# ConvFFN up-projection: weight sums and token operands between VectorE and GpSimd, and the PSUM banks of the GLA's output projection

## The chip, the cores and the metric

The kernel runs on one NeuronCore of a Trainium2 chip. Its engines are TensorE (matmuls), VectorE, ScalarE and GpSimd (element-wise work), and SyncE, which issues the DMAs. Each engine works through its own queue in order, and semaphores make one wait for another. The metric is the device time of one execution in microseconds (us), the median of several runs. "PE", "DVE", "ACT", "POOL" and "SP" in the profile are TensorE, VectorE, ScalarE, GpSimd and SyncE; "PEld" is TensorE's weight load.

## The reference

Two layers of a hybrid diffusion backbone in float32 over 1024 latent tokens and 256 context tokens, D = 1024. Layer 0 mixes tokens by a Fourier mixer beside a bidirectional gated linear attention (GLA), layer 1 by grouped-query attention; each is followed by a ConvFFN. What matters here:

```python
def conv_ffn(h, w_up, w_conv, b_conv, w_down):
    u = dwconv_centred(h @ w_up, w_conv, b_conv)     # 1024 -> 2 x 2816, three taps over tokens
    g, v = jnp.split(u, 2, axis=-1)
    return (jax.nn.silu(g) * v) @ w_down

# layer 0
y = jnp.concatenate([fourier_mix(u_f), o], axis=-1) @ w_out      # o: output of the GLA
h_lat = h_lat + ga1 * o_lat
f_lat = rms_norm(h_lat, g_norm_ffn[i]) * (1 + sc2) + sh2
h_lat = h_lat + ga2 * conv_ffn(f_lat, w_ffn_up[i], w_ffn_conv[i], b_ffn_conv[i], w_ffn_down[i])
```

## The kernel before, in words

**Products in three matmuls.** Each float32 operand is split into a high part, a rounded copy made by ScalarE (`split`, L208), and a low part, the subtraction that is left (`tt`, L204). A product is three matmuls of such parts (`mm3`): low times high, high times low, high times high. A group of matmuls needs the low part first, so it waits for the subtraction, which runs on VectorE (`V`) or GpSimd (`G`) as the call of `split` says.

**FFN up.** The product `h @ w_up` is a 2 x 2 block product in seven multiplications instead of eight (`PRODS`). Its token operands (B11, T1, B21, B22, T2, T4, T3) are blocks of the normed tokens and differences of them. `ffn_ops` makes them once for each half of the tokens (`hf` 0 and 1; n = 640 tokens a half in layer 0, 512 in layer 1; each block has u = n/2 columns). Its weight operands (A11, S1, A12, S2, S4, A22, S3) are made for each of the 22 blocks of 128 columns (f). `Up.load` loads two tiles of 8 x 128 columns (L1217), `Up.sums` makes three sums of halves of them, and `Up.split` makes the difference for S4 and splits all seven. All these are instructions on 128x512 elements. One (f, which halves) is a visit; layer 0 has 25 and layer 1 has 24, most of them over both halves.

**One step** (`up_step`) is one f and one half: seven groups of 12 matmuls into four PSUM banks X, V, W and Z. X takes A11's group, is copied out by ScalarE (L1307), and goes on accumulating with S2's group, so S2's first matmul waits for that copy. The other copies and additions out of PSUM (L1309 to L1319) are ScalarE's and VectorE's. `up_conv` then does the convolution of the step before: ScalarE's L1333 (centre tap) and L1335 (SiLU), and two VectorE instructions for the other taps (L1338 and L1339, or L1343 and L1345). The columns go to DRAM (L1352).

**Buffers.** The weights use ten slots (`W`): seven operands of the visit in work, and the two loaded tiles and the sums of the next. A slot comes free when the last half has used an operand, and `pump` then lets the next visit's work go on.

**Before the first FFN up** the GLA's half of the output projection runs (`out_part(4, 4, ...)`): for each half and each of the eight blocks n two PSUM tiles of 320 columns, each of 12 matmuls. VectorE adds each tile to the residual stream (`resid`, L918), which frees its bank. The banks go round in the group `MB = (0, 3)`, the first three; the first FFN-up visits go round in the group (0, 5). After each block of the second half, `h_done` does two steps of `ffn_ops` for the first half; those for the second half run as `side` within FFN up. Layer 1 has the same in `att_out(1, first)`, the attention's output projection, beside `ffn_ops` of the first half and the first visits' weights.

**What sets the order.** In the FFN TensorE's order is that of the code (`manual_schedule`). VectorE, ScalarE, GpSimd and the DMAs are ordered by a planner, which goes by the streams' priorities, the order of the code and its own reckoning of when each instruction is ready.

Of the kernel before, what the change touches and what calls it, by code (L numbers as in the profile page):

```python
# [15 lines left out]
ALU = mybir.AluOpType  # L16
# [88 lines left out]
def tile_hybrid_dit(  # L105
# [12 lines left out]
    V = nc.vector  # L118
    A = nc.scalar
    G = nc.gpsimd  # L120
# [82 lines left out]
    def tt(out_, a, b, op, eng=None):  # L203
        return (eng or V).tensor_tensor(out_, a, b, op)  # L204
# [39 lines left out]
    MB, XB, GB = (0, 3), (3, 1), (4, 4)  # L244
# [898 lines left out]
    def ffn_ops(N, ops, ring_p=None):  # L1143

        u = N.n // 2

        def put(name, p, src, eng):
            b = S((2, 2, u), True)
            split(src, b[:, 0], b[:, 1], eng)
            ops[name][p] = b  # L1150
        t0, t1 = N.hp[:2], N.hp[2:]
        b11, b12, b21, b22 = [[t[:, :, i * u:(i + 1) * u] for t in ts] for ts in (t0, t1) for i in range(2)]
        for p in range(2):
            N.scale(p)
            yield
            N.scale(p + 2)
            yield
            put("B11", p, b11[p], G)
            yield
        for p in range(2):  # L1160
            tt(b11[p], b12[p], b11[p], ALU.subtract)
            put("T1", p, b11[p], V)
            yield
        for p in range(2):
            put("B21", p, b21[p], G)
            yield
        for p in range(2):
            ring_t = [SM(2 * u).rearrange("p (k n) -> p k n", k=2) for _ in range(1)] if p == ring_p else None
            put("B22", p, b22[p], V)
            t3 = ring_t[0] if ring_t else b12[p]  # L1170
            tt(t3, b22[p], b12[p], ALU.subtract, G)
            yield
            tt(b22[p], b22[p], b11[p], ALU.subtract)
            put("T2", p, b22[p], V)
            yield
            if ring_t:
                t0[p].free()
                put("T3", p, t3, G)
                yield
                t4 = SM(2 * u).rearrange("p (k n) -> p k n", k=2)  # L1180
                tt(t4, b21[p], b22[p], ALU.subtract)
                t1[p].free()
                put("T4", p, t4, G)
            else:
                tt(b21[p], b21[p], b22[p], ALU.subtract)
                put("T4", p, b21[p], G)
                t1[p].free()
                yield
                put("T3", p, b12[p], G)
                t0[p].free()  # L1190
            yield
# [11 lines left out]
    class Up:  # L1203
# [18 lines left out]
        def sums(self):  # L1222
            r, tmp = self.r, self.tmp
            lo, hi = slice(0, 4), slice(4, 8)
            e = self.sum_on
            tt(tmp[:, lo], r[1][:, lo], r[1][:, hi], ALU.add, e)
            tt(tmp[:, hi], tmp[:, lo], r[0][:, lo], ALU.subtract, e)
            tt(r[1][:, lo], r[0][:, lo], r[1][:, lo], ALU.subtract, e)

        def split(self, M):  # L1230

            r, tmp = self.r, self.tmp
            lo, hi = slice(0, 4), slice(4, 8)
            src = dict(A11=r[0][:, lo], S2=tmp[:, hi], S3=r[1][:, lo], S1=tmp[:, lo], A12=r[0][:, hi], A22=r[1][:, hi], S4=r[0][:, lo])
            for a, _, _ in PRODS:
                b = M((2, 4, P), True)
                split(src[a], b[:, 0], b[:, 1], V if a in self.on_v else G)
                self.w[a] = b
                if a == "A11":
                    tt(r[0][:, lo], r[0][:, hi], tmp[:, hi], ALU.subtract, G)  # L1240
                elif a == "S2":
                    tmp.free()
                elif a == "S3":
                    r[1].free()
                elif a == "S4":
                    r[0].free()
                yield

    V1 = (("S3", "S1", "A12"), ("S3", "S1", "A12"))
    V2 = (("S3", "S1", "A12"), ("S3", "S1", "A12"))  # L1250
    S1 = (G, G)

    class Ups:


        def __init__(self, l, single):
            self.visits = [(f, (0,)) for f in range(single)]
            for f in range(single, NF):
                self.visits.append((f, (0, 1)))
                if f < 2 * single:  # L1260
                    self.visits.append((f - single, (1,)))
            self.made = [Up(l, f) for f, _ in self.visits]
            for i, up in enumerate(self.made):
                up.on_v, up.sum_on = (V1[l], S1[l]) if i < 2 * single + 1 else (V2[l], G)
            self.gen = self.prep(self.made[1:], W)

        def prep(self, ups, M, after=None):
# [394 lines left out]
    with stream(1):  # L1662
        for hf in range(2):
            go_load(hf)
            go_dump(0, hf)
            go_dump(1, hf)
        S.join(GM)
        run(ups.prep(ups.made[:1], S, gl[1, 1].f[:, 1, HALF - 1:HALF]))
        out_part(4, 4, lambda k, hf: (gh[k // 2, hf][:, k % 2, :], gl[k // 2, hf][:, k % 2, :]), MB, h_done,
                 lambda: pump(ups.gen, (W, 1)))  # L1670
    if "mem" in dbg:
        print("least S", S.low, "W", W.low, "GM", GM.low)
# [447 lines left out]
```

## Time and profile before

| | |
|---|---|
| time, median of 3 runs | 3104.79 us (3103.47 to 3115.6) |
| the profiled execution | 3111.55 us, its span 3109.8 us |
| TensorE busy | 2812.2 us, 90% |
| VectorE busy | 2332.2 us, 75% |
| ScalarE busy | 1448.9 us, 47% |
| GpSimd busy | 1535.5 us, 49% |
| first FFN up | about 722 to 1330 us |
| second FFN up | about 2310 to 2830 us |

All times within the kernel are from the start of the span of the profiled execution. A busy share is a mean over the span. In a row of a timeline, "[2.09 <-ACT t L1307]" says that the engine stood idle for 2.09 us before the instruction and that ScalarE's line 1307 ended the wait; "x3" says that three instructions of one kind followed each other without a gap. L204 is the line of the helper `tt` and L208 that of `split`'s copy, so most element-wise work carries these two lines, and one tells the instructions apart by engine, shape and time.

### The profile page before, as it was taken

How to read it: one execution, taken by the hardware profiler on the slowest of the kernel's cores; microseconds unless marked ns; L12 is line 12 of the kernel's file. 1: busy time of each engine (PE TensorE's matmuls, PEld its weight loads, DVE VectorE, ACT ScalarE, POOL GpSimd, SP SyncE). 2: the span in 40 equal slices, each digit the busy share in tenths (PEclk: the TensorE clock that was granted, in tenths of full speed). 3: DMA queues.
4: the chain of work that ended last, by engine and by line, in shares of the span. 5: the costliest groups of instructions: out<-in, count | busy, mean ns of one | idle time of the engine just before them, and what ended most of it. 6: DMA issues, size and time to landing. Idle time of an engine off the chain costs nothing. (4 is left out here: it accounts for less than half of the span.)

```text
span 3109.8 us, 52191 instructions
## 1 busy us (share of the span) xinstructions
PE 2812.2 (90%) x20047; PEld 2680.2 (86%) x20047; DVE 2332.2 (75%) x3729; ACT 1448.9 (47%) x2896; POOL 1535.5 (49%) x1229
## 2 busy tenths in 40 slices
PE   6999987897899999997989899999977999998888
PEld 3999977796899999997989889989867989998788
DVE  7897489869776666768674788868788778887774
ACT  3544433435444444442353546646655444544333
POOL 2025273127554444467874753343377555554661
PEclk7999978898999999998999999999998999999899
DMA  8553202321344434387733220020231222228763
GB/s 275 180 167 100 96 31 94 127 99 48 104 141 128 128 110 128 100 268 233 246 108 116 89 82 11 28 92 21 75 92 58 78 73 67 77 77 272 235 214 108
DMA packets 375790, 371.28 MB, mean 119 GB/s; under 512 B 15579, under 2 KB 305011, under 8 KB 375540
## 3 DMA queue, kind: packets, MB, share of 16 engines
q1 hardware_dynamic: 374482, 365.88, 37.1%
q8 instruction: 157, 2.57, 0.3%
q10 hardware_dynamic: 1058, 2.07, 0.2%
q14 instruction: 93, 0.76, 0.1%
HBM read 282.95 MB, written 84.93 MB: 118 GB/s over the span
## 5 line engine op out<-in xcount | busy, mean ns | idle before, releaser
L154 PE MATMUL psum<-t,t 128*128 128x256 f32 (+4 forms) x17896 | 2615.2, 306 | 208.2 <-DVE t L204 77.5
L154 PEld LDWEIGHTS psum<-t,t 128*128 128x128 f32 x17896 | 2490.8, 196 | 296.6 <-DVE t L204 91.0
L204 POOL TENSOR_TENSOR t<-t,t 128x512 fp32r<-128x512 f32 (+8 forms) x736 | 1077.6, 1479 | 866.1 <-ACT t L208 523.3
L204 DVE TENSOR_TENSOR t<-t,t 128x512 fp32r<-128x512 f32 (+13 forms) x760 | 808.8, 1092 | 168.3 <-ACT t L208 123.6
L208 ACT CAST t<-t 128x512 fp32r<-128x512 f32 (+5 forms) x857 | 555.4, 670 | 648.8 <-POOL t L204 182.9
L204 POOL TENSOR_TENSOR t<-t 128x512 f32<-128x512 f32 (+3 forms) x265 | 327.7, 1254 | 390.4 <-ACT t L664 157.4
L204 DVE TENSOR_TENSOR t<-t,psum 128x320 f32<-128x320 f32 (+4 forms) x416 | 202.9, 508 | 126.4 <-PE psum L154 94.3
L1333 ACT ACTIVATE t<-t,cvs 128x639 f32<-128x639 f32 (+3 forms) x176 | 153.1, 870 | 153.4 <-DVE t L204 142.5
L208 ACT CAST t<-psum 128x512 fp32r<-128x512 f32 (+4 forms) x248 | 130.7, 536 | 134.2 <-PE psum L158 60.0
L158 PE MATMUL psum<-ident,t 128*128 128x128 f32 (+2 forms) x955 | 150.9, 280 | 38.7 <-DVE t L204 23.4
L1918 POOL TENSOR_SCALAR t<-t,ring 128x640 f32<-128x640 f32 x128 | 101.6, 807 | 170.4 <-DVE ring L1908 80.7
L204 DVE TENSOR_TENSOR t<-psum,t 128x512 fp32r<-128x512 f32 (+4 forms) x248 | 151.3, 615 | 37.0 <-ACT t L208 33.9
L158 PEld LDWEIGHTS psum<-ident,t 128*128 128x128 f32 (+2 forms) x955 | 113.1, 143 | 47.8 <-DVE t L204 27.6
L918 DVE SCALAR_TENSOR_TENSOR t<-psum,mods,t 128x256 f32<-128x256 f32 (+2 forms) x208 | 91.9, 473 | 62.7 <-PE psum L154 53.2
L1907 DVE TENSOR_REDUCE ring<-psum 128x1 f32<-128x640 f32 x128 | 104.5, 817 | 20.0 <-PE psum L154 14.4
L1909 ACT ACTIVATE t<-psum,ring 128x640 f32<-128x640 f32 x128 | 102.3, 800 | 25.6 <-DVE ring L1908 11.9
L1335 ACT ACTIVATE t<-t 128x511 f32<-128x511 f32 (+3 forms) x88 | 60.4, 686 | 82.2 <-DVE t L1339 45.7
L204 DVE TENSOR_TENSOR ring<-ring 128x1 f32<-128x1 f32 (+5 forms) x296 | 76.2, 259 | 20.8 <-ACT ring L1912 12.8
L1313 ACT COPY t<-psum 128x320 f32<-128x320 f32 (+1 forms) x88 | 35.2, 400 | 121.2 <-PE psum L154 121.2
L1338 DVE SCALAR_TENSOR_TENSOR t<-t,cvs 128x641 f32<-128x641 f32 (+1 forms) x44 | 52.0, 1182 | 47.3 <-ACT t L1333 47.3
L1343 DVE SCALAR_TENSOR_TENSOR t<-t,cvs 128x255 f32<-128x255 f32 (+1 forms) x66 | 53.7, 840 | 44.5 <-ACT t L1333 44.5
L338 DVE SCALAR_TENSOR_TENSOR t<-t,scv,t 128x256 f32<-128x256 f32 x168 | 80.1, 527 | 3.1 <-DMA t<-in_w_mod_dram 2.9
(144 smaller groups left out, 1672.7 us busy)
## 6 DMA issues: line engine op xcount, KB each, us to landing
t<-in_w_ffn_up_dram SPq DMA_DIRECT2D x98, 512.0 KB, 3.9
ring<-in_w_mod_dram SPq DMA_DIRECT2D x56, 512.0 KB, 4.0
t<-in_w_ffn_down_dram SPq DMA_DIRECT2D x96, 256.0 KB, 5.5
t<-in_w_even_in_dram SPq DMA_DIRECT2D x28, 512.0 KB, 4.7
t<-in_w_ffn_down_dram SPq DMA_DIRECT2D x72, 192.0 KB, 3.8
t<-y_d SPq DMA_DIRECT2D x20, 640.0 KB, 5.9
t<-in_w_mod_dram SPq DMA_DIRECT2D x96, 128.0 KB, 2.2
t<-in_w_ffn_down_dram SPq DMA_DIRECT2D x24, 512.0 KB, 4.5
```

The costliest lines, as they stand in the source:

```text
L154: cls.keep(out_, nc.tensor.matmul(out_, *args, **kw).ins)
L158: cls.keep(out_, nc.tensor.transpose(out_, *args).ins)
L204: return (eng or V).tensor_tensor(out_, a, b, op)
L208: A.copy(hi, src)
L338: behind(V.scalar_tensor_tensor(a, r, s, a, ALU.mult, ALU.add))
L918: last_resid[0] = V.scalar_tensor_tensor(h[:, n % 2, a:b], ps[:, a - c0:b - c0], mods[:, l, m, n, v:v + 1], h[:, n % 2, a:b], ALU.mult, AL ...
L1333: A.activation(x, c[:, j, at:at + m], AF.Identity, bias=tap(l, 3, ft), scale=tap(l, 1, ft))
L1335: A.activation(us[0], us[0], AF.Silu)
L1343: V.scalar_tensor_tensor(x[:, s0 + 1:e], c[:, j, 2 + s0:1 + e], tap(l, 0, ft), x[:, s0 + 1:e], ALU.mult, ALU.add)
L1907: V.tensor_reduce(mx[:, i:i + 1], ps, AX.XY, ALU.max)
L1909: A.activation(pt[:, i * HALF:(i + 1) * HALF].rearrange("p (b n) -> p b n", b=2), ps, AF.Exp, bias=nb[:, i:i + 1], scale=SCALE, accum_out= ...
L1918: G.tensor_scalar(pt[:, i * HALF:(i + 1) * HALF], pt[:, i * HALF:(i + 1) * HALF], ex[:, i:i + 1], 1.0, ALU.mult, ALU.mult)
```

## The change

In `Up.sums` the three weight sums go from GpSimd to VectorE, and so does the difference for S4 in `Up.split`. Which weight splits run on VectorE is now one list, `ON_V`, in place of lists by layer and visit; it names the same three operands as these did. In `ffn_ops` the split of B11, the difference for T3 and the split of T4 go from GpSimd to VectorE, and the split of B22 from VectorE to GpSimd. The GLA's output projection takes its PSUM tiles from the group (0, 5) in place of (0, 3).

```diff
--- before.py
+++ after.py
@@ -1155,7 +1155,7 @@
             yield
             N.scale(p + 2)
             yield
-            put("B11", p, b11[p], G)
+            put("B11", p, b11[p], V)
             yield
         for p in range(2):
             tt(b11[p], b12[p], b11[p], ALU.subtract)
@@ -1166,9 +1166,9 @@
             yield
         for p in range(2):
             ring_t = [SM(2 * u).rearrange("p (k n) -> p k n", k=2) for _ in range(1)] if p == ring_p else None
-            put("B22", p, b22[p], V)
+            put("B22", p, b22[p], G)
             t3 = ring_t[0] if ring_t else b12[p]
-            tt(t3, b22[p], b12[p], ALU.subtract, G)
+            tt(t3, b22[p], b12[p], ALU.subtract)
             yield
             tt(b22[p], b22[p], b11[p], ALU.subtract)
             put("T2", p, b22[p], V)
@@ -1180,10 +1180,10 @@
                 t4 = SM(2 * u).rearrange("p (k n) -> p k n", k=2)
                 tt(t4, b21[p], b22[p], ALU.subtract)
                 t1[p].free()
-                put("T4", p, t4, G)
+                put("T4", p, t4, V)
             else:
                 tt(b21[p], b21[p], b22[p], ALU.subtract)
-                put("T4", p, b21[p], G)
+                put("T4", p, b21[p], V)
                 t1[p].free()
                 yield
                 put("T3", p, b12[p], G)
@@ -1222,10 +1222,9 @@
         def sums(self):
             r, tmp = self.r, self.tmp
             lo, hi = slice(0, 4), slice(4, 8)
-            e = self.sum_on
-            tt(tmp[:, lo], r[1][:, lo], r[1][:, hi], ALU.add, e)
-            tt(tmp[:, hi], tmp[:, lo], r[0][:, lo], ALU.subtract, e)
-            tt(r[1][:, lo], r[0][:, lo], r[1][:, lo], ALU.subtract, e)
+            tt(tmp[:, lo], r[1][:, lo], r[1][:, hi], ALU.add)
+            tt(tmp[:, hi], tmp[:, lo], r[0][:, lo], ALU.subtract)
+            tt(r[1][:, lo], r[0][:, lo], r[1][:, lo], ALU.subtract)
 
         def split(self, M):
 
@@ -1234,10 +1233,10 @@
             src = dict(A11=r[0][:, lo], S2=tmp[:, hi], S3=r[1][:, lo], S1=tmp[:, lo], A12=r[0][:, hi], A22=r[1][:, hi], S4=r[0][:, lo])
             for a, _, _ in PRODS:
                 b = M((2, 4, P), True)
-                split(src[a], b[:, 0], b[:, 1], V if a in self.on_v else G)
+                split(src[a], b[:, 0], b[:, 1], V if a in ON_V else G)
                 self.w[a] = b
                 if a == "A11":
-                    tt(r[0][:, lo], r[0][:, hi], tmp[:, hi], ALU.subtract, G)
+                    tt(r[0][:, lo], r[0][:, hi], tmp[:, hi], ALU.subtract)
                 elif a == "S2":
                     tmp.free()
                 elif a == "S3":
@@ -1246,9 +1245,7 @@
                     r[0].free()
                 yield
 
-    V1 = (("S3", "S1", "A12"), ("S3", "S1", "A12"))
-    V2 = (("S3", "S1", "A12"), ("S3", "S1", "A12"))
-    S1 = (G, G)
+    ON_V = ("S1", "A12", "S3")
 
     class Ups:
 
@@ -1260,8 +1257,6 @@
                 if f < 2 * single:
                     self.visits.append((f - single, (1,)))
             self.made = [Up(l, f) for f, _ in self.visits]
-            for i, up in enumerate(self.made):
-                up.on_v, up.sum_on = (V1[l], S1[l]) if i < 2 * single + 1 else (V2[l], G)
             self.gen = self.prep(self.made[1:], W)
 
         def prep(self, ups, M, after=None):
@@ -1666,7 +1661,7 @@
             go_dump(1, hf)
         S.join(GM)
         run(ups.prep(ups.made[:1], S, gl[1, 1].f[:, 1, HALF - 1:HALF]))
-        out_part(4, 4, lambda k, hf: (gh[k // 2, hf][:, k % 2, :], gl[k // 2, hf][:, k % 2, :]), MB, h_done,
+        out_part(4, 4, lambda k, hf: (gh[k // 2, hf][:, k % 2, :], gl[k // 2, hf][:, k % 2, :]), (0, 5), h_done,
                  lambda: pump(ups.gen, (W, 1)))
     if "mem" in dbg:
         print("least S", S.low, "W", W.low, "GM", GM.low)
```

## Rows read from the trace of the kernel before

**Rows 1.** Busy time by stretch: the stretch and its length in us, then for each engine busy us and (x instructions), the granted TensorE clock as a share of full speed, the share of the DMA engines and GB/s.

```profile
690.00:734.00 44.00, 30.17 (x160) 28.59 (x160) 34.43 (x36) 24.65 (x42) 31.38 (x18) 0.84 0.16 57
734.00:802.00 68.00, 49.03 (x268) 47.05 (x268) 60.01 (x71) 37.30 (x60) 45.37 (x30) 0.80 0.17 54
802.00:1330.00 528.00, 524.93 (x3730) 490.12 (x3730) 372.54 (x496) 246.01 (x437) 247.16 (x208) 1.00 0.39 124
2250.00:2340.00 90.00, 69.01 (x370) 59.57 (x369) 73.94 (x72) 50.60 (x87) 72.77 (x46) 0.90 0.29 89
2340.00:2800.00 460.00, 419.02 (x3366) 414.20 (x3366) 369.86 (x432) 222.78 (x436) 267.35 (x215) 0.97 0.24 73
```

**Rows 2.** TensorE's waits, by who ended them: us in total, times, longest. The first row is of 690 to 734 us, the second of 734 to 802, the third of 2250 to 2340, the last two of 2340 to 2800.

```profile
PE psum L154 <- DVE t L918: 13.8, 4, 6.2
...
PE psum L154 <- POOL t L204: 10.4, 4, 4.4
...
PE psum L154 <- POOL t L204: 10.3, 5, 4.9
...
PE psum L154 <- ACT t L1307: 24.5, 15, 2.4
PE psum L154 <- POOL t L204: 12.9, 5, 3.4
```

**Rows 3.** Timeline of one visit of the second FFN up and the change to the next, 2581 to 2604 us: start, duration, engine, line, operation, tiles, shape, count, and the idle time before it with what ended it.

```profile
2581.24 0.38 SPq L1217 DMA_DIRECT2D t<-in_w_ffn_up_dram  x1
...
2585.11 3.01 POOL L204 TENSOR_TENSOR t<-t,t 128x512 f32<-128x512 f32 x2 [3.90 <-DMA t<-in_w_ffn_up_dram]
...
2591.06 1.89 DVE L1345 SCALAR_TENSOR_TENSOR t<-t,cvs 128x511 f32<-128x511 f32 x1
2591.09 4.70 POOL L204 TENSOR_TENSOR t<-t,t 128x512 fp32r<-128x512 f32 x3 [1.59 <-ACT t L208]
...
2592.86 3.48 DVE L204 TENSOR_TENSOR t<-t,t 128x512 fp32r<-128x512 f32 x2
...
2596.59 0.68 DVE L204 TENSOR_TENSOR t<-t,t 128x512 fp32r<-128x512 f32 x1
...
2599.33 1.66 DVE L1339 SCALAR_TENSOR_TENSOR t<-t,cvs,t 128x512 f32<-128x512 f32 x1
...
2601.02 0.63 ACT L1335 ACTIVATE t<-t 128x513 f32<-128x513 f32 x1 [1.73 <-DVE t L1339]
2601.32 1.26 POOL L204 TENSOR_TENSOR t<-t 128x512 f32<-128x512 f32 x1 [0.88 <-DVE t L204]
...
2602.78 0.35 ACT L1307 COPY t<-psum 128x256 f32<-128x256 f32 x1
...
2603.28 0.95 PE L154 MATMUL psum<-t,t 128*128 128x256 f32 x6 [2.09 <-ACT t L1307]
```

**Rows 4.** Groups of instructions by line and shape, 2340 to 2800 us: first GpSimd's sums of weights (three of a visit's four have the first form, the sum of two halves of one tile has the second), then three of VectorE's groups. Behind the count: busy us, mean ns of one, and the engine's idle time before them with what ended it.

```profile
L204 POOL TENSOR_TENSOR t<-t,t 128x512 f32<-128x512 f32 x63 | 96.1, 1539 | 91.7 <-DMA t<-in_w_ffn_up_dram 90.2
L204 POOL TENSOR_TENSOR t<-t 128x512 f32<-128x512 f32 x20 | 25.8, 1290 | 15.5 <-DMA t<-in_w_ffn_up_dram 7.4 <-DVE t L204 4.3 <-DVE t L1339 2.9
...
L204 DVE TENSOR_TENSOR t<-t,t 128x512 fp32r<-128x512 f32 x67 | 73.0, 1090 | 3.8 <-ACT t L208 3.8
...
L204 DVE TENSOR_TENSOR t<-t,t 128x511 f32<-128x511 f32 x20 | 34.5, 1723 | 0.0
L1345 DVE SCALAR_TENSOR_TENSOR t<-t,cvs 128x511 f32<-128x511 f32 x20 | 31.7, 1586 | 0.7
```

**Rows 5.** Timeline of the change from the output projection to the first FFN up, 700 to 733 us, columns as in rows 3.

```profile
700.67 1.57 POOL L204 TENSOR_TENSOR t<-t,t 128x640 fp32r<-128x640 f32 x1 [0.94 <-ACT t L208]
...
704.75 15.50 POOL L204 TENSOR_TENSOR t<-t,t 128x640 fp32r<-128x640 f32 x8
...
722.00 11.39 PE L154 MATMUL psum<-t,t 128*128 128x320 f32 x60 [6.18 <-DVE t L918]
...
725.01 0.81 DVE L204 TENSOR_TENSOR t<-t 128x640 f32<-128x640 f32 x1
...
725.71 4.79 POOL L204 TENSOR_TENSOR t<-t,t 128x512 fp32r<-128x512 f32 x3 [3.38 <-ACT t L208]
```

**Rows 6.** GpSimd's plain 128x512 differences and sums by shape, columns as in rows 4: two rows of 690 to 734 us, two of 734 to 802, two of 2250 to 2340.

```profile
L204 POOL TENSOR_TENSOR t<-t,t 128x512 f32<-128x512 f32 x3 | 5.4, 1805 | 0.0
...
L204 POOL TENSOR_TENSOR t<-t 128x512 f32<-128x512 f32 x1 | 1.8, 1796 | 0.8 <-DVE t L204 0.8
...
L204 POOL TENSOR_TENSOR t<-t,t 128x512 f32<-128x512 f32 x6 | 8.7, 1457 | 4.0 <-DMA t<-in_w_ffn_up_dram 3.9
L204 POOL TENSOR_TENSOR t<-t 128x512 f32<-128x512 f32 x3 | 5.0, 1682 | 10.0 <-DVE t L1345 7.1 <-DMA t<-in_w_ffn_up_dram 2.9
...
L204 POOL TENSOR_TENSOR t<-t,t 128x512 f32<-128x512 f32 x12 | 18.6, 1563 | 4.2 <-DMA t<-in_w_ffn_up_dram 2.1 <-DVE t L204 1.9
...
L204 POOL TENSOR_TENSOR t<-t 128x512 f32<-128x512 f32 x4 | 5.6, 1394 | 1.0 <-DMA t<-in_w_ffn_up_dram 1.0
```

**Rows 7.** Waits in 2340 to 2800 us by who ended them, columns as in rows 2: GpSimd's for weights, and VectorE's two for ScalarE.

```profile
POOL t L204 <- DMA t<-in_w_ffn_up_dram: 97.6, 29, 6.6
...
DVE t L1343 <- ACT t L1333: 34.8, 38, 1.1
DVE t L1338 <- ACT t L1333: 29.4, 34, 1.3
```

## The prediction

> **What bounds the kernel now.** The shares of the page (table above) are means over stages with different limits, so I begin with the busy times by stretch, over the two FFN-up stages and what leads into them [rows 1]. They show four different limits. In the steady part of the first FFN-up (802 to 1330 us) TensorE is busy 524.9 of 528 us: nothing that happens on VectorE or GpSimd there can be won back. In the run-up to it (690 to 734 and 734 to 802) TensorE idles 13.8 and 19.0 us, at granted clocks of 0.84 and 0.80. In the run-up to the second FFN-up (2250 to 2340) it idles 21.0 us, and in the second FFN-up itself (2340 to 2800), whose matmuls are 256 columns wide instead of 320, 41.0 us. Together that is 94.8 us, and it is all that the change can reach.
>
> Second view, who ends TensorE's waits in each stretch [rows 2]: between 690 and 734 it is the residual add on VectorE (L918), 13.8 us in four waits; between 734 and 802 and between 2250 and 2340 GpSimd ends 10.4 and 10.3 us; in the second FFN-up ScalarE's L1307 ends 24.5 us in 15 waits and GpSimd 12.9 us in five.
>
> L1307 copies the A11 product out of PSUM and takes 0.35 us, so it isn't slow itself. The third view, the timeline of one change of visit, shows why it is late [rows 3]: ScalarE works in order, L1307 (2602.78) stands behind L1335 (2601.02), L1335 has waited 1.73 us for the convolution on VectorE (L1339, 1.66 us), and before that VectorE had run contended splits since 2591.06. The two engines slow each other: a subtraction or product on 512 columns takes VectorE 0.68 us when GpSimd is idle (2596.59) and 1.74 us when it runs (2592.86, two in 3.48 us); it takes GpSimd 1.26 us alone and 1.57 us beside it (2591.09, three in 4.70 us). A pair that alone would cost 0.68 + 1.26 = 1.94 us takes 1.57 to 1.74 us together, 81% to 90% of the sum. I take 85%: what the two engines do between SBUF tiles goes nearly one after the other. So in these stretches it is the sum over both engines that counts, and VectorE does the same work in about half the time.
>
> The Trainium skill (SBUF — State Buffer, section "SBUF: two separate sides") says of this that VectorE instructions with two SBUF inputs and GpSimd instructions take a shared pair of ports as an exclusive lock for the whole instruction, so the sum would count in full. The rows show a little less than that; by the page the total below would be 38 us instead of 32, still the same case.
>
> **The change part by part.** *Weight operands.* Each visit prepares one column block of weights: three sums, a fourth difference for S4, and seven splits. Today the four sums run on GpSimd, of the splits A11, S2, S4 and A22 too, and S3, S1, A12 on VectorE. The new list of splits names the same three, so no split moves: GpSimd goes from eight instructions a visit to four, VectorE gets four more. The rows count them: in 2340 to 2800, 63 + 20 = 83 sums of 128x512 in plain f32 [rows 4], 20.75 visits. Each moved sum takes 1.26 us off GpSimd and puts 0.68 us on VectorE; of the shared time that saves 0.58 x 0.85 = 0.49 us.
>
> In the second FFN-up not all four count. Two of them (2585.11, x2) run in the half of the visit where TensorE doesn't wait; the first sum (2601.32) and the S4 difference (one of the three at 2591.09) lie in the loaded stretch that ends with TensorE's 2.09 us wait [rows 3]. So 2 x 0.49 = 0.98 us a visit, x 20.75 = 20 us, of the 41.0 us there. GpSimd's own five waits (12.9 us) should go as well, since its queue is half as long, but they are in the same 41 us and I don't add them. Bounds: nothing, or all of the 41 us; a loss is the third rival's.
>
> In the first FFN-up's steady part I take 0: TensorE hides it. Its cover is large: VectorE is busy 372.5 of 528 us there [rows 1], 71%.
>
> *Token operands.* Of the seven operands per half, B11's split, the T3 difference and T4's split go to VectorE and B22's split goes to GpSimd. There are two of each (p = 0, 1), so GpSimd loses a net four instructions per half and VectorE gets them. In the first layer they are 128x640: 1.57 us on GpSimd at 700.67, and 0.81 us on VectorE at 725.01 [rows 5]; each saves 0.76 x 0.85 = 0.65 us of shared time. In 690 to 734 there are also 3 + 1 weight sums, in 734 to 802 another 6 + 3 [rows 6]. That gives 4 x 0.65 + 4 x 0.49 = 4.6 us and 4 x 0.65 + 9 x 0.49 = 7.0 us, 11.6 us together. GpSimd is close to saturated there (eight instructions without a gap from 704.75, 15.5 us [rows 5]) and TensorE idles 32.8 us, but not every instruction lies ahead of one that it waits for; I take two thirds, 8 us. Bounds: 0 and 20.
>
> In 2250 to 2340 there are 12 + 4 plain differences [rows 6], T3's among them, and a net two splits: 18 x 0.49 = 8.8 us. GpSimd ends half of TensorE's idle time there (10.3 of 21.0), since the attention output weights are split behind this work. I take half, 4 us, between 0 and 10.
>
> *Five PSUM banks.* The GLA's part of the output projection uses banks 0 to 4 instead of 0 to 2, the group from which FFN-up then takes its own. A tile then waits for the L918 five tiles before it, not three. The four waits, 13.8 us, should mostly go, that at 722.00 (6.18 us) included. But TensorE only runs ahead to the next obstacle: the first visit of FFN-up needs all seven token operands, and the last GpSimd splits for it end at 730.5 (725.71 + 4.79) [rows 5], while TensorE gets through most of that visit by 733.4 (722.00 + 11.39). So by themselves the banks are worth 0 to 5 us; I count nothing beyond the 8 us.
>
> Sum: 20 + 8 + 4 = 32 us. The profiled execution took 3111.55 us, 1.75 us beyond its span of 3109.8 us; 3111.55 - 32 = 3079.6. The median of the runs is 6.8 us lower than the profiled one, so I forecast 3104.8 - 32 = 3073 us. Clock that comes back when the gaps close isn't counted.
>
> **The rivals.** *All of it comes.* If the two engines had been the only limit, TensorE saturates in the second FFN-up too: 41 us there, 11.6 + 8.8 us in the run-ups, 3044 us. For it: GpSimd's and L1307's waits have one origin. Against it: VectorE stays about as busy as before, and its queue is what L1307 waits for.
>
> *VectorE keeps what GpSimd gives up.* Four more instructions a visit are 4 x 0.68 = 2.7 us of VectorE time. What it gains is less contention: the 67 split subtracts at 1.09 us, the 20 products at 1.72 us and the 20 L1345 at 1.59 us [rows 4] lie above the 0.68 us of a free one by 27 + 21 + 18 = 66 us, 3.2 us a visit; with half of GpSimd's instructions gone, half of it, 1.6 us. By this count VectorE's load grows by 1.1 us a visit and the critical queue is no shorter; only the run-ups gain, 12 us: 3093 us, no change.
>
> *VectorE stands still for weights (slower).* The sums are the first readers of the loaded weights. GpSimd now waits 97.6 us for in_w_ffn_up in this stretch [rows 7], 4.7 us a visit, at no cost. On VectorE a sum at the head of the queue holds up the PSUM adds and the convolution behind it, ScalarE's L1333, L1335 and L1307 wait for those, and TensorE for L1307. VectorE has 369.9 / 20.75 = 17.8 us of work in a visit of 460 / 20.75 = 22.2 us; with 1.1 us more, and the 3.1 us that it already waits for L1333 (34.8 + 29.4 us [rows 7]), 22.0 us are spoken for. A new wait of more than about 1 us a visit decides. If half of GpSimd's wait, 2.35 us, lands there and half of that is absorbed, it costs 1.2 x 20.75 = 24 us; up to 45 us if none is. Less 12 us in the run-ups that is 3117 to 3138, say 3127 us. For it: the load lands 3.9 us after its issue (2581.24 to 2585.11 [rows 3]). Against it: VectorE has gaps of its own in each visit, those before L1333's results, into which the sums can fall, and the planner orders by what its own reckoning says is ready. The first layer has room for such a wait.
>
> *That the planner, which orders every engine but TensorE here, moves something unrelated* can add or take some 10 us to any of these.
>
> **How the numbers follow.** My case (about 3073, its own range 3058 to 3088) has 0.45, all of it 0.15, VectorE keeps it 0.23, VectorE waits 0.17. About 0.5%, 15.5 us, is what a measurement can tell from no change, so faster means under 3089 and slower over 3120. The first two are faster; of the second rival a tenth or so is faster by chance, and of the third a quarter stays within the band: faster 0.62, same 0.24, slower 0.14. The range 3036 to 3118 leaves out the far end of the first rival and the upper half of the third.
>
> **What would show it.** Right: in the second FFN-up GpSimd's instructions halve, TensorE's waits for GpSimd are gone, those for L1307 fall to about half, and the mean of VectorE's 128x512 split falls from 1.09 towards 0.8 us; in 690 to 734 no waits for L918; in 802 to 1330 no difference. Wrong: rows in which VectorE waits for in_w_ffn_up by more than 20 us in total; TensorE's waits for L1307 as long as before; or a difference in stages that the change does not touch.

## The result, and the profile after

The kernel after takes 3085.54 us (median of 6 runs, 3078.85 to 3093.69) beside 3106.18 us for the kernel before on the same chip: ratio 0.9929 [0.9913, 0.9945], about 22 us. The forecast was 3073 us, 3058 to 3088 for the likeliest case. The profiled execution took 3089.33 us, its span 3087.4 us.

Where the 22.3 us between the two spans come from, by the start of the same instruction in both traces (the copies of A11's product, L1307 before and L1302 after, are numbered from 0 in each FFN up, two per visit):

| stretch | before, us | after, us | difference | forecast |
|---|---|---|---|---|
| middle of the output projection to copy 10 of the first FFN up | 632.0 to 890.9 | 632.1 to 880.4 | -10.6 | -8 |
| from there to its last copy, 43 | to 1342.0 | to 1330.2 | -1.2 | 0 |
| to copy 10 of the second FFN up | to 2445.3 | to 2417.8 | -15.7 | -4 |
| to its copy 43 | to 2814.0 | to 2792.1 | **+5.6** | **-20** |
| to the end | to 3109.8 | to 3087.4 | -0.5 | 0 |

So the sum is near, but the two run-ups bring 26 us instead of 12, and the steady second FFN up, which should have brought most, has become slower. (The forecast's 20 us were for 2340 to 2800 us, 20.75 visits; copies 10 to 43 are 16.5 visits, for which the same 0.98 us a visit make 16 us.) The busy times by stretch of the kernel after, which answer to [rows 1], the stretches moved with the stage:

```profile
690.00:734.00 44.00, 32.05 (x178) 30.73 (x177) 39.38 (x52) 28.17 (x47) 23.59 (x10) 0.78 0.21 69
734.00:802.00 68.00, 51.76 (x318) 50.48 (x317) 63.41 (x89) 39.94 (x66) 26.24 (x20) 0.87 0.17 54
802.00:1320.00 518.00, 515.18 (x3668) 480.78 (x3667) 369.82 (x568) 242.15 (x430) 123.35 (x122) 1.00 0.39 125
2236.00:2326.00 90.00, 67.86 (x370) 58.88 (x369) 75.64 (x88) 51.36 (x86) 48.22 (x30) 0.89 0.29 89
2326.00:2786.00 460.00, 425.97 (x3418) 420.06 (x3416) 376.73 (x531) 225.00 (x447) 134.78 (x129) 0.97 0.26 79
```

GpSimd's instructions fall to about six tenths: of a visit's eight on the weights four are left, and its other work has stayed. In the steady first FFN up TensorE is busy 515.2 of 518 us, as before. TensorE's waits, which answer to [rows 2], the first row of 690 to 734 us, the second of 734 to 802, the third of 2236 to 2326, the last two of copies 10 to 43 of the second FFN up:

```profile
PE psum L154 <- DVE t L204: 11.9, 4, 4.5
...
PE psum L154 <- DVE t L204: 14.4, 2, 8.3
...
PE psum L154 <- POOL t L204: 12.0, 4, 7.4
...
PE psum L154 <- ACT t L1302: 22.2, 19, 2.0
PE psum L154 <- DVE t L204: 5.2, 1, 5.2
```

The waits for L918 and, in the first run-up, for GpSimd are gone; waits for VectorE's L204, which makes the operands now, stand in their place. In the second run-up GpSimd still ends 12.0 us. In the second FFN up the waits for GpSimd are gone too, but those for the A11 copy are not: 22.2 us, against 23.7 us in the same copies before. The same 33 copies in one row each, the kernel before first (columns as in [rows 1]):

```profile
2445.30:2814.00 368.70, 339.73 (x2750) 336.72 (x2751) 297.66 (x354) 179.57 (x354) 195.98 (x165) 0.97 0.26 79
```

```profile
2417.80:2792.10 374.30, 346.53 (x2771) 342.30 (x2770) 298.99 (x422) 178.98 (x357) 99.75 (x102) 0.96 0.26 80
```

GpSimd's busy time has halved; VectorE does 68 instructions more and is as busy as before, 299.0 and 297.7 us. What it lost in contention has paid for the sums, and no more. By groups (2400 to 2790 us, for [rows 4]):

```profile
L204 DVE TENSOR_TENSOR t<-t,t 128x512 fp32r<-128x512 f32 x57 | 50.4, 886 | 0.0
L204 DVE TENSOR_TENSOR t<-t,t 128x512 f32<-128x512 f32 x51 | 34.3, 701 | 26.7 <-DMA t<-in_w_ffn_up_dram 26.7
L1340 DVE SCALAR_TENSOR_TENSOR t<-t,cvs 128x511 f32<-128x511 f32 x17 | 30.8, 1812 | 0.6
L204 DVE TENSOR_TENSOR t<-t,t 128x511 f32<-128x511 f32 x17 | 20.3, 1196 | 0.0
```

A split has fallen from 1.09 to 0.89 us and the 511 product from 1.72 to 1.20, but L1340 (before: L1345) has risen from 1.59 to 1.81 us. The second row shows the sums at their free 0.70 us, and a wait for weights that VectorE did not have before. One visit of it, in the timeline (columns as in [rows 3]):

```profile
2580.77 1.29 DVE L204 TENSOR_TENSOR t<-t,t 128x512 f32<-128x512 f32 x2 [2.18 <-DMA t<-in_w_ffn_up_dram]
...
2582.44 0.81 ACT L1328 ACTIVATE t<-t,cvs 128x511 f32<-128x511 f32 x1 [4.28 <-DVE t L204]
...
2587.21 1.89 DVE L1340 SCALAR_TENSOR_TENSOR t<-t,cvs 128x511 f32<-128x511 f32 x1
2587.25 1.30 POOL L204 TENSOR_TENSOR t<-t,t 128x512 fp32r<-128x512 f32 x1 [1.60 <-ACT t L208]
...
2589.03 2.38 DVE L204 TENSOR_TENSOR t<-t,t 128x512 fp32r<-128x512 f32 x2
2589.39 1.46 POOL L204 TENSOR_TENSOR t<-t,t 128x512 fp32r<-128x512 f32 x1 [0.84 <-ACT t L208]
...
2591.66 1.28 DVE L204 TENSOR_TENSOR t<-t,t 128x512 f32<-128x512 f32 x2
...
2594.76 1.35 POOL L204 TENSOR_TENSOR t<-t,t 128x512 fp32r<-128x512 f32 x1 [3.90 <-ACT t L208]
2594.99 1.66 DVE L1334 SCALAR_TENSOR_TENSOR t<-t,cvs,t 128x512 f32<-128x512 f32 x1
...
2596.69 0.63 ACT L1330 ACTIVATE t<-t 128x513 f32<-128x513 f32 x1 [1.74 <-DVE t L1334]
...
2597.24 0.68 DVE L204 TENSOR_TENSOR t<-t 128x512 f32<-128x512 f32 x1
...
2598.45 0.35 ACT L1302 COPY t<-psum 128x256 f32<-128x256 f32 x1
...
2598.94 1.40 PE L154 MATMUL psum<-t,t 128*128 128x256 f32 x5 [2.03 <-ACT t L1302]
```

This is the picture of [rows 3] once more: L1302 behind L1330, L1330 behind VectorE's tap L1334, and that stretched to 1.66 us by one of GpSimd's splits. What GpSimd gave up were the sums; its four splits of weights are still there, and each runs in part beside a VectorE instruction.

### The profile page after: what moved, and what is told of

It is laid out like the page before. It is cut to its first block, busy times and chain, and to the rows that moved or that the text cites. A ratio compares the mean times of both kernels' runs of the same rounds, so it can differ in the third digit from the quotient of the medians.

```text
span 3087.4 us, 52053 instructions
## 1 busy us (share of the span) xinstructions
PE 2798.3 (91%) x20047; PEld 2667.7 (86%) x20047; DVE 2342.0 (76%) x3941; ACT 1446.6 (47%) x2896; POOL 1218.0 (39%) x1017
## 5 line engine op out<-in xcount | busy, mean ns | idle before, releaser
L154 PE MATMUL psum<-t,t 128*128 128x256 f32 (+3 forms) x17896 | 2601.8, 305 | 197.4 <-DVE t L204 98.9
L204 POOL TENSOR_TENSOR t<-t,t 128x512 fp32r<-128x512 f32 (+7 forms) x577 | 831.3, 1453 | 986.4 <-ACT t L208 799.5
L204 DVE TENSOR_TENSOR t<-t,t 128x512 fp32r<-128x512 f32 (+12 forms) x919 | 866.5, 976 | 184.9 <-ACT t L208 113.9
L208 ACT CAST t<-t 128x512 fp32r<-128x512 f32 (+5 forms) x857 | 555.9, 670 | 644.8 <-DVE t L204 158.7
L204 POOL TENSOR_TENSOR t<-t 128x320 f32<-128x320 f32 (+2 forms) x216 | 265.1, 1248 | 262.4 <-ACT t L664 157.1
L204 DVE TENSOR_TENSOR t<-t,psum 128x320 f32<-128x320 f32 (+4 forms) x416 | 203.1, 508 | 85.8 <-PE psum L154 64.8
L1328 ACT ACTIVATE t<-t,cvs 128x639 f32<-128x639 f32 (+3 forms) x176 | 153.1, 870 | 179.8 <-DVE t L204 167.5
L208 ACT CAST t<-psum 128x512 fp32r<-128x512 f32 (+4 forms) x248 | 130.6, 535 | 136.6 <-PE psum L158 61.2
L204 DVE TENSOR_TENSOR t<-psum,t 128x512 fp32r<-128x512 f32 (+4 forms) x248 | 151.3, 615 | 37.5 <-ACT t L208 34.8
L1318 POOL COPY halo<-t 128x4 f32<-128x4 f32 x44 | 9.1, 207 | 403.5 <-DVE t L204 403.5
L918 DVE SCALAR_TENSOR_TENSOR t<-psum,mods,t 128x256 f32<-128x256 f32 (+2 forms) x208 | 92.2, 475 | 59.0 <-PE psum L154 49.6
L204 DVE TENSOR_TENSOR t<-t 128x128 f32<-128x128 f32 (+3 forms) x167 | 88.5, 558 | 21.8 <-DMA t<-in_w_ffn_up_dram 19.5
L1330 ACT ACTIVATE t<-t 128x511 f32<-128x511 f32 (+3 forms) x88 | 60.2, 684 | 72.7 <-DVE t L1334 40.3
L204 DVE TENSOR_TENSOR ring<-ring 128x1 f32<-128x1 f32 (+5 forms) x296 | 72.6, 247 | 21.3 <-ACT ring L1907 13.3
```

The source lines that it names most:

```text
L154: cls.keep(out_, nc.tensor.matmul(out_, *args, **kw).ins)
L208: A.copy(hi, src)
L918: last_resid[0] = V.scalar_tensor_tensor(h[:, n % 2, a:b], ps[:, a - c0:b - c0], mods[:, l, m, n, v:v + 1], h[:, n % 2, a:b], ALU.mult, AL ...
L1328: A.activation(x, c[:, j, at:at + m], AF.Identity, bias=tap(l, 3, ft), scale=tap(l, 1, ft))
L1330: A.activation(us[0], us[0], AF.Silu)
```

## The experiments

Two questions were open: what failed in the steady second FFN up, and which parts make the run-ups. Medians are of 4 to 10 runs, beside 13 to 27 of the kernel before (3110.0 to 3112.5 us) on the same chip. "Steady" is copies 10 to 43 of the second FFN up, 368.7 us before and 374.3 after; "run-up 1" and "run-up 2" are the first and third line of the table above. In the kernel after and four others with its first layer, run-up 1 came out between -10.6 and -11.2 us, so differences there are good to about 1 us; in run-up 2 two kernels with one and the same second layer lie 6.6 us apart (weights alone, weights and banks), and in the steady part two others 5.8 us (tokens alone, tokens and banks). There a smaller difference is read only where whole groups of kernels show it. The stretches are of the one profiled execution of each kernel.

**One part alone: weights.** The kernel before with this edit:

```diff
-            e = self.sum_on
-            tt(tmp[:, lo], r[1][:, lo], r[1][:, hi], ALU.add, e)
+            tt(tmp[:, lo], r[1][:, lo], r[1][:, hi], ALU.add)
...
-                    tt(r[0][:, lo], r[0][:, hi], tmp[:, hi], ALU.subtract, G)
+                    tt(r[0][:, lo], r[0][:, hi], tmp[:, hi], ALU.subtract)
```

> Only the weight sums and the S4 difference go to VectorE; token operands and banks as before. Theory A (the weight sums make the gain in the run-ups and cost a little in the steady second FFN-up): 3092 us, of it 5 us won ahead of the first FFN-up's 20th step, 12 us between the end of the first FFN-up and the second one's 10th step, and 5 us lost from there to its end. Rival B (token operands and banks make the gain): within 5 us of before, since the steady second FFN-up loses what little the run-ups win.

3113.65 us, 1.0016 [0.9994, 1.0037]. Run-up 1 +3.3, run-up 2 -1.4, steady 373.5 us. Theory A misses but for the loss in the steady part; the total is as rival B has it.

**Tokens alone** (the hunks at lines 1155 to 1183):

> Only the token operands (B11, T3, T4 to VectorE, B22 to GpSimd). Theory A: 4 us less, 2 in each run-up, nothing in the steady stages. Rival B: 10 to 15 us less, in both run-ups.

3111.83 us, 0.9996 [0.9975, 1.0016]. Run-up 1 +1.1, run-up 2 +0.6, steady 368.9. Both ideas miss: there is no gain.

**Banks alone** (`MB` to `(0, 5)`):

> Only five PSUM banks for the GLA's part of the output projection. Theory A: TensorE's waits for L918 between 690 and 734 us (13.8 us) go, and come back as waits for the token operands right behind them; 0 to 3 us less in total, and the second layer as before. Rival B: most of the 13.8 us stay won, 10 us less.

3105.84 us, 0.9969 [0.9951, 0.9987]. The first FFN up begins 13.1 us earlier, and by copy 10 1.4 us of that are left: between 690 and 734 us TensorE no longer waits for L918, but 15.4 us for L204 and L208, which make operands. Run-up 2 -1.0, steady 370.7. That is theory A's account; the total, 4.6 us less by the medians, lies between the two ideas. No part alone brings what the change brings.

**The kernel after, with layer 1's sums back on GpSimd:**

```diff
+            e = G if self.l else V
-            tt(tmp[:, lo], r[1][:, lo], r[1][:, hi], ALU.add)
+            tt(tmp[:, lo], r[1][:, lo], r[1][:, hi], ALU.add, e)
...
-                    tt(r[0][:, lo], r[0][:, hi], tmp[:, hi], ALU.subtract)
+                    tt(r[0][:, lo], r[0][:, hi], tmp[:, hi], ALU.subtract, G if self.l else V)
```

> The changed kernel with the second layer's sums and S4 difference back on GpSimd. Theory A: the steady second FFN-up (10th to 43rd step) takes 368.7 us as before, not 374.3, the run-up to it loses 10 us; 3090 us. Rival C (the sums on VectorE don't matter in the second layer, the token operands do): 3085 us, the 10th step of the second FFN-up as early as in the changed kernel.

3099.48 us, 0.9942 [0.9918, 0.9966]. Steady 365.6 us, 8.7 less than the kernel after; run-up 1 as there (-10.6), run-up 2 +2.0 instead of -15.7, more than theory A's 10 us. Moving layer 1's sums to VectorE costs in the steady part and pays in the run-up.

**Pairs.** Weights and tokens without the banks (the kernel after with `MB`):

> The changed kernel with three PSUM banks again: weight sums and token operands together. Theory D (in the run-ups TensorE needs both queues; a part done alone only moves the wait to the other queue, so the two must be done together): 13 to 18 us less than before, of it 8 ahead of the first FFN-up's 10th step and 14 more by the second one's 10th step. Rival E (the three parts are each worth what they show alone, and the rest of the changed kernel's gain is in the banks' making room): within 5 us of before.

3097.23 us, 0.9966 [0.9948, 0.9984]. Run-up 1 -1.2, run-up 2 -17.1, steady 372.8. The banks, worth 1.4 us alone, are worth 9.4 us of run-up 1 on top of the other two. So theory D's total is near (12.8 us less by the medians), but its 8 us ahead of the first FFN up are not there without the banks. Weights and banks, tokens as before:

> Weight sums on VectorE and five banks, token operands as before. Theory D: no more than the banks alone, 0 to 4 us less than before. Rival E: 10 us less by the first FFN-up's 10th step.

3108.33 us, 1.0000 [0.9982, 1.0018]. Run-up 1 -0.5, run-up 2 -8.0, steady 372.6: theory D, not rival E. Tokens and banks, the weights as before:

> The kernel before with the changed token operands and the five banks, and nothing of the weights: the one pair not yet run. Theory (the first layer's gain needs all three parts): the run-up to the first FFN up gains 0 to 3 us, the second FFN up none, 3100 to 3108 us. Rival (tokens and banks are what the first layer needs, the weight sums count only in the second): the run-up gains 10 us, 3093 to 3098 us.

3099.69 us, 0.9961 [0.9939, 0.9983]. Run-up 1 -7.4: both ideas miss. The pair of tokens and banks makes most of run-up 1 (-7.4 against +1.1 and -1.4 alone), and the weights, useless without it, add 3 us. Run-up 2 +2.0, so there the tokens bring nothing without the weights; steady 363.1.

**Is it the wait for weights?** The kernel after, where in layer 1 the second and third sum, which read the tile that lands late, go back to GpSimd:

```diff
+            e = G if self.l else V
             tt(tmp[:, lo], r[1][:, lo], r[1][:, hi], ALU.add)
-            tt(tmp[:, hi], tmp[:, lo], r[0][:, lo], ALU.subtract)
-            tt(r[1][:, lo], r[0][:, lo], r[1][:, lo], ALU.subtract)
+            tt(tmp[:, hi], tmp[:, lo], r[0][:, lo], ALU.subtract, e)
+            tt(r[1][:, lo], r[0][:, lo], r[1][:, lo], ALU.subtract, e)
```

> The changed kernel, but in the second layer the two sums that read the late load (the second and third) run on GpSimd; the first sum and the S4 difference stay on VectorE. Theory A (in the steady second FFN-up VectorE's wait for weights, 28.5 us, is what ate the gain): from the 10th to the 43rd step 360 us instead of 374, no VectorE wait for in_w_ffn_up. Rival F (VectorE's queue is as full as before whoever does the sums, since what it no longer loses to GpSimd it spends on the sums): 366 to 374 us, TensorE's waits for the A11 copy as long as before.

3082.72 us, 0.9921 [0.9894, 0.9948]. Run-up 1 -11.1, run-up 2 -2.3: what the steady part gains here, the run-up gives back, and as a whole this kernel is no faster than the kernel after (0.9929). VectorE's wait for the weights in the kernel after (2400 to 2790 us):

```profile
DVE t L204 <- DMA t<-in_w_ffn_up_dram: 28.5, 18, 2.3
```

and in this one (2420 to 2790), with its steady row:

```profile
DVE t L204 <- DMA t<-in_w_ffn_up_dram: 0.2, 1, 0.2
...
2433.50:2793.40 359.90, 332.52 (x2749) 329.36 (x2750) 299.49 (x384) 178.55 (x354) 148.07 (x134) 0.99 0.26 81
```

The wait is gone and the steady part is 14.4 us shorter, theory A's 360 us. VectorE's busy time is the same, 299.5 us against 299.0. But one thing is as rival F has it: TensorE idles as long as in the kernel after, 359.9 - 332.5 = 27.4 us against 374.3 - 346.5 = 27.8. What differs is how long it is busy with the same matmuls, and with it the granted clock, 0.99 against 0.96. In the kernel after, around one of TensorE's 2.0 us waits:

```profile
2462.00:2465.70 3.70, 1.70 (x15) 1.52 (x14) 3.00 (x6) 2.38 (x5) 1.26 (x1) 1.00 0.00 0
2465.70:2469.10 3.40, 3.40 (x19) 3.40 (x18) 1.79 (x4) 0.37 (x1) 0.00 (x0) 0.50 0.74 231
```

TensorE idles for 2.0 us, and about 1 us after the wait 3.4 us run at 0.50, 1.2 GHz instead of 2.4, with half the work of 3.4 us at full speed: 1.7 us lost. Is that the 14.4 us, and the wait for weights only its occasion? Two visits of the kernel after that follow each other, from the copy that begins one to the copy that begins the next, without and with such a stretch, and a visit of this kernel:

```profile
2531.12:2553.41 22.29, 20.27 (x168) 20.09 (x168) 17.78 (x25) 10.42 (x23) 5.81 (x7) 1.00 0.24 71
2553.41:2575.59 22.18, 21.69 (x168) 21.55 (x168) 17.70 (x25) 10.77 (x22) 5.69 (x7) 0.92 0.23 72
```

```profile
2540.93:2562.49 21.56, 20.23 (x168) 20.06 (x168) 17.86 (x23) 10.60 (x23) 9.01 (x9) 1.00 0.24 74
```

The visit at half speed is no longer. What TensorE loses by the clock it waits less: it idles 0.5 us in place of 2.0. And with the two sums back the visit is 0.7 us shorter at the same clock and with the same VectorE time. The means over the 16 visits from copy 10 to copy 42 of each kernel say the same; the second step of a visit, in which GpSimd's splits run, is called the loaded one:

| kernels | first step, us | loaded step, us | visits all at full speed | visits with a half-speed stretch |
|---|---|---|---|---|
| sums on GpSimd in layer 1: before, tokens, banks, layer-1 sums, tokens and banks | 9.53 | 12.53 | 62, mean 21.80 us | 18, mean 22.94 us |
| sums on VectorE: after, weights, weights and tokens, weights and banks | 10.29 | 12.13 | 37, mean 22.48 | 27, mean 22.33 |
| two sums back: late sums | 9.64 | 11.94 | 16, mean 21.58 | none |

With the sums on VectorE its queue sets the length of a visit, whatever TensorE's clock: the waiting sums hold the first step up by some 0.7 us a visit, more than the 0.4 us by which the loaded step becomes shorter. So it is the wait for weights that costs the 14.4 us, 0.9 us a visit, and the half-speed stretches there take the place of idle time. (With the sums on GpSimd the visits with such a stretch are 1.1 us longer; there part of it may be the clock's.)

**Is it GpSimd's splits?** The kernel after with all seven splits of layer 1 on VectorE:

```diff
-                split(src[a], b[:, 0], b[:, 1], V if a in ON_V else G)
+                split(src[a], b[:, 0], b[:, 1], V if self.l or a in ON_V else G)
```

> The changed kernel with all seven weight splits of the second layer on VectorE, so that GpSimd does next to nothing in the steady second FFN-up. If the sum over both engines counts (my prediction's reckoning), four more moved instructions save 4 x 0.49 = 2 us a visit: 340 to 350 us from the 10th to the 43rd step instead of 374. If VectorE's in-order queue counts (rival F): no gain or a loss, 374 to 400 us, although its splits all take 0.68 us.

3039.98 us, 0.9779 [0.9746, 0.9813]. The steady row, and VectorE's split of 128x512 (2380 to 2740 us):

```profile
2409.60:2743.60 334.00, 330.45 (x2774) 330.24 (x2774) 278.19 (x483) 184.33 (x355) 11.01 (x37) 1.00 0.28 88
...
L204 DVE TENSOR_TENSOR t<-t,t 128x512 fp32r<-128x512 f32 x131 | 88.5, 691 | 18.8 <-ACT t L208 18.8
```

VectorE does 61 instructions more than in the kernel after and is busy 20.8 us less; a split takes 0.69 us without a neighbour. TensorE idles 3.6 us. Rival F falls. The reckoning by the sum comes near, but this kernel can't tell the sum from the place.

**The sum over both engines, or the place?** The halves exchanged: as the last kernel, and layer 1's sums and S4 difference on GpSimd, by the same edit as in "layer 1's sums back on GpSimd".

> The kernel after with layer 1's halves exchanged: all seven weight splits on VectorE, the three sums and the difference for S4 back on GpSimd. GpSimd has four 128x512 instructions of a visit as in the kernel after, only others. Theory of the sum (what counts is how much runs on both engines together, whichever instructions they are): the steady part of the second FFN up takes 365 to 376 us as in the kernel after (374.3), about 3085 us. Theory of the place (what counts is which instructions VectorE waits for: sums at the head of its queue wait for the loads, and loads wait for GpSimd's last split of a visit): with the splits on VectorE and the waiting on GpSimd it takes 336 to 350 us, 3045 to 3060 us.

3049.56 us, 0.9805 [0.9763, 0.9847]. Its steady row:

```profile
2417.50:2751.80 334.30, 330.91 (x2771) 330.70 (x2770) 279.06 (x421) 185.52 (x356) 109.76 (x101) 0.99 0.28 88
```

This decides it. VectorE has 421 instructions and GpSimd 101, where the kernel after has 422 and 102; GpSimd is even busier (109.8 us against 99.8); and the stage takes 334.3 us instead of 374.3. Not how much runs on both engines counts, but where it stands. Four kernels with the same first layer, token operands and banks give the price of each half:

| steady part, us | splits A11, S2, S4, A22 on GpSimd | all splits on VectorE |
|---|---|---|
| sums and S4 difference on GpSimd | 365.6 | 334.3 |
| on VectorE | 374.3 | 334.0 |

The four splits make 31 to 40 us. Where the sums stand counts only beside GpSimd's splits. With all splits on VectorE it makes no difference, though in one of the two kernels VectorE still waits for weights, 8.5 us. So the reason that the theory of the place gave, sums that wait at the head of VectorE's queue, is not what makes these 31 to 40 us. The two steps of one visit, from copy to copy of A11, in the kernel after:

```profile
2575.59:2586.30 10.71, 10.24 (x85) 10.04 (x84) 6.63 (x11) 3.42 (x8) 1.11 (x3) 1.00 0.24 75
2586.30:2598.45 12.15, 10.21 (x84) 10.01 (x84) 11.09 (x14) 7.00 (x15) 4.66 (x4) 1.00 0.23 67
```

and with the halves exchanged, the loaded step first:

```profile
2567.23:2576.66 9.43, 9.43 (x82) 9.43 (x81) 9.27 (x14) 6.14 (x13) 1.73 (x1) 1.00 0.24 77
2576.66:2587.55 10.89, 10.89 (x94) 10.89 (x93) 7.94 (x12) 4.91 (x10) 4.77 (x5) 1.00 0.26 80
```

In the loaded step VectorE has 14 instructions in both kernels, but in one four splits of GpSimd stand beside them and in the other a single difference. The three sums fall into the other step, where VectorE has 3 us to spare:

```profile
2568.14 0.69 DVE L204 TENSOR_TENSOR t<-t,t 128x512 fp32r<-128x512 f32 x1
...
2573.58 1.28 DVE L204 TENSOR_TENSOR t<-t,t 128x512 fp32r<-128x512 f32 x2
...
2576.16 0.75 DVE L1335 SCALAR_TENSOR_TENSOR t<-t,cvs,t 128x512 f32<-128x512 f32 x1
2576.66 0.38 ACT L1303 COPY t<-psum 128x256 f32<-128x256 f32 x1 [0.88 <-PE psum L154]
...
2579.77 1.30 POOL L204 TENSOR_TENSOR t<-t 128x512 f32<-128x512 f32 x1 [9.13 <-DMA t<-in_w_ffn_up_dram]
...
2581.38 3.10 POOL L204 TENSOR_TENSOR t<-t,t 128x512 f32<-128x512 f32 x2 [0.32 <-DMA t<-in_w_ffn_up_dram]
```

The A11 copy now waits for TensorE, not TensorE for it, and GpSimd's 9.13 us of waiting for weights cost nothing. As means over 14 visits (each instruction counted whole in the step in which it starts, so that the sum can exceed the length; "stretch" is VectorE's time over that of the same instructions without GpSimd):

| loaded step | length | VectorE busy | of it stretch | GpSimd busy |
|---|---|---|---|---|
| before | 12.53 us | 11.54 | 4.17 | 8.36 |
| after | 12.15 | 11.94 | 3.20 | 5.40 |
| halves exchanged | 9.35 | 10.32 | 1.10 | 1.73 |

**All splits on VectorE in both layers:**

```diff
-                split(src[a], b[:, 0], b[:, 1], V if a in ON_V else G)
+                split(src[a], b[:, 0], b[:, 1], V)
```

> The kernel after with all seven weight splits on VectorE in both layers, so that GpSimd does nothing for the weights. Theory (what a second engine does between SBUF tiles costs VectorE about as much as doing it itself, and all that is moved away from GpSimd shortens the queue that TensorE waits for): the second FFN up as with the splits of the second layer alone, the run-up to the first FFN up a few us shorter than that, 3032 to 3042 us. Rival (in the run-up of the first FFN up VectorE is already the last, and each further split there is 0.7 us more of TensorE's wait): the run-up longer by 5 to 10 us, 3044 to 3052 us.

3031.84 us, 0.9744 [0.9696, 0.9793]. Run-up 1 -17.3 us, 6.6 better than the kernel after and the four others with its first layer; steady 334.3. The rival falls. It is the fastest kernel of the study, 2.6% below the kernel before and 1.7% below the kernel after (3031.84 / 3085.54, from two sets of runs); its interval overlaps that of all splits in layer 1 alone, and what sets it apart from that one is run-up 1. That it is the faster of these two as a whole is not shown: their profiled executions take 3043.5 and 3042.2 us.

## Why the prediction was right, and where it was wrong

**The total.** 3085.5 us lies 12.5 us above the forecast and inside the likeliest case's own range, but its terms were 8 + 4 + 20 and came out as 11 + 16 - 6. That the total is so near is luck: the run-ups were 14 us too small and the steady part 26 us too large. Right was that the gain is in the run-ups and the second layer and none in the steady first FFN up.

**The step that failed** is the 20 us of the steady second FFN up: "it is the sum over both engines that counts", 0.98 us a visit saved by the two sums in the loaded stretch, and nothing for the other two. The kernel with the halves exchanged has as many instructions on both engines and is 40 us faster there. What counts is VectorE's queue from one A11 copy to the next. In the loaded step the second rival's account holds, "VectorE keeps what GpSimd gives up": the change took 4.17 - 3.20 = 0.97 us of contention away and put two more instructions in, 2 x 0.69 = 1.4 us, and VectorE's busy time there went from 11.54 to 11.94 us. The step became shorter all the same, but by 0.38 us and not by 0.98. The other two sums, which I had put at nothing because TensorE doesn't wait in their half of the visit, made that half some 0.7 us longer. So the change lost 0.3 us a visit where I had 0.98 us won.

The rows had told it. In [rows 3], GpSimd's 4.70 us beside VectorE's 3.48 us were three instructions, of which two are splits: in the loaded stretch most of GpSimd's work was splits, and the change left all four of them there. I halved GpSimd's instructions and with them, in thought, the contention; the half that went was the half that did less harm.

**The third rival**, VectorE standing still for weights, came true in its mechanism. VectorE waits 28.5 us for the weights (I had set 20 us as the mark of being wrong), and ScalarE's L1328 behind it 4.28 us in the visit shown. Taking two of the sums back removed the wait, and the steady part became 14.4 us shorter, 0.9 us a visit where the rival had 1.2. Against the kernel before the loss is only 5.6 us, because the two sums in the loaded stretch, which stayed on VectorE, gain: with them alone moved the steady part is 359.9 us, below all five kernels with the sums on GpSimd (363.1 to 370.7). The sum's 16 us for them came out as 6 to 9 (365.6 and 368.7 to 359.9), little more than two kernels with one second layer differ by. The clock is not what the loss is made of. Of TensorE's eight waits of 1.9 to 2.0 us in the kernel after seven are followed by a half-speed stretch, but a visit with one is as long as a visit without. Why some waits bring the drop and others don't stays open: in the kernel with the two sums back one of 2.0 us brought none, and in the kernel before neither did two of 2.0 and 2.2 us, while one of 1.8 us was followed by one.

**The run-ups.** Run-up 1 was sized 8 us and measured 10.6. The banks by themselves were put at 0 to 5 us, with nothing counted beside the token operands: alone they bring 1.4 us, for the reason given (TensorE runs ahead and meets the next operands), but the two belong together, -7.4 us as a pair. Either wait covers the other, so parts that are worth 1.4 us at best one by one add up to 10.6. Run-up 2 was sized 4 us and measured 15.7. Most of that, 13.7 us, comes after the middle of the attention's output projection (2245.5 us before, 2231.7 after): up to copy 10 TensorE's idle time fell from 36.7 to 31.5 us and its time at half speed from 34.1 to 23.9 us, 5.2 + 5.1 = 10.3 us together. So 5 of the 13.7 us may be the clock, which I had left out of the sum, and 3 us I can't place. It takes the weights and the tokens: tokens without the weight sums bring +0.6 and +2.0 us, weight sums without the tokens -1.4 and -8.0, both -15.7 and -17.1. But it needn't be the sums: with the halves exchanged, where the splits moved in their place, it is -14.3.

**The signs named beforehand.** Right: GpSimd's work on the weights halved; waits for GpSimd gone from the steady part; waits for L918 gone; no difference in the steady first FFN up. Half right: the split's mean fell to 0.89 us, not 0.8. Wrong: the waits for L1307 did not fall to half, 23.7 to 22.2 us, and VectorE's wait for weights passed its mark.

## What to carry to other kernels

When two engines slow each other, don't add up their work; take the one queue and the one stretch that sets the wait, list what the other engine runs beside it instruction by instruction, and move exactly that. Work that waits for loads is better kept out of the queue that sets the pace: here that was worth 14.4 us as long as VectorE's queue did so, and nothing once it no longer did (334.0 and 334.3 us). And where two waits cover each other, test the parts in pairs before any of them is dropped as useless.

## What the runs showed of the hardware

Work that VectorE took over from GpSimd cost it less than nothing: with 61 instructions more in the steady part, VectorE's busy time fell from 299.0 to 278.2 us.

The contention is not shared evenly. In the first run-up of the kernel after, one of GpSimd's splits of 128x640 takes 7.03 us, where it takes 1.57 us in [rows 5]:

```profile
717.03 7.03 POOL L204 TENSOR_TENSOR t<-t,t 128x640 fp32r<-128x640 f32 x1 [4.52 <-ACT t L208]
...
715.33 5.83 DVE L204 TENSOR_TENSOR t<-t,t 128x640 f32<-128x640 f32 x8
...
722.54 0.48 DVE L204 TENSOR_TENSOR t<-t,psum 128x320 f32<-128x320 f32 x1
722.94 1.80 DVE L204 TENSOR_TENSOR t<-t,t 128x640 fp32r<-128x640 f32 x1
```

Before and beside it VectorE ran eight instructions back to back, one every 5.83 / 8 = 0.73 us, not slowed. The Trainium skill (SBUF — State Buffer, section "SBUF: two separate sides") has the one that starts first hold the shared ports for its whole instruction while the other is blocked; these rows agree with the blocking, and show in addition that GpSimd did not get in between VectorE's instructions on SBUF tiles while those came without a gap. Its split ends at 724.06, 1.5 us after VectorE had come to one that reads PSUM (722.54), and the VectorE split behind that is the one that is slowed, 1.80 us. In [rows 3] and in the visit above it is VectorE that is slowed, although L1345 and L1340 start 0.03 and 0.04 us ahead of GpSimd's split by the profile; these rows don't show that the first one wins. What decides which of the two loses, no run here was made to find.
